# A scan with reciprocals inside its second running products, one mask operation, and its weights split in the early stage

## The chip, the cores and the metric

The kernel runs on one core of a Trainium2 chip. The metric is the device time of one execution, in microseconds. Before the change it is 2709.33 us, the median of 3 runs (2708.7 to 2710.57). TensorE is called PE here, VectorE DVE, ScalarE ACT, GpSimd POOL and SyncE SP; SP issues nearly all DMAs.

## The reference

One layer of a diffusion trunk over 2048 tokens of width 1024, with 256 context tokens ahead: an adaptive norm, an HGRN2 mixer with 8 heads in both directions, and a gated convolution FFN. The change is in the mixer's scan, for a head (cut):

```python
f = lb[d] + (1.0 - lb[d]) * jax.nn.sigmoid(zf)      # k = 1 - f, logf = log f
b = jnp.cumsum(logf, axis=3)                        # over chunks of 64 tokens
qe = q * jnp.exp(b - b_ref)
ke = k * jnp.exp(b_ref - b)
scores = jnp.where(mask, einsum('bhnik,bhnjk->bhnij', qe, ke), 0.0)
o_intra = einsum('bhnij,bhnjv->bhniv', scores, v)
kv = einsum('bhnjk,bhnjv->bhnkv', k * jnp.exp(b_last - b), v)
s = decay[..., None] * s + kv                       # from chunk to chunk
o_inter = einsum('bhnik,bhnkv->bhniv', q * jnp.exp(b), s_start)
```

The latent scans start from the state that the context leaves.

## The kernel before

The program is written out in order, stage by stage, and every engine works through its own instructions in order; a wait at the head of an engine's queue holds up all that is behind it. Work beside the matmuls is put at due times: `tick()` counts one for each three matmuls of a projection (`step`, L937), `at(when, f)` asks for `f` at such a count.

**Early stage** (`early`, L253, to 554.9 us of the trace). Projections of q and v in a scheme with fewer products on quadrants of the token matrix (names such as T2, B12). Matmuls are fp32r in three parts: a number x is split (`split`, L79) into a high half h, a copy on ACT (L80), and the rest l, a subtraction on DVE (L81). From the product `turn_over` on, a generator `ada_rest` (L716) does side work at due times, one step every 7 ticks, 37 steps: it streams rows of the modulation weights through a ring `spare` of four 128 x 1024 slots, multiplies on DVE (L732) and writes rows to DRAM (L746). `spare`, `fraw` (raw factors, loaded at L758 and split later into `rT`, `rB` or `tok`) and `cxt` (the context's modulated tokens, 2 MB, loaded at L1328) are tiles of one tag, "cxt", with a single buffer: each may be filled only when all uses of its forerunner are done. At the last use of T2 the generator is run to its end, and the block B12 is loaded through `fraw` and split into `tok`. The last results of the stage pass a Silu on ACT (L528) and go to DRAM.

**Scan** (`mixer_scan`, L897, 554.9 to 1203 us). Twice (g = 0, 1: the halves of the tokens) over 8 heads; a head has two units of four 128-token tiles, and in g = 0 the context first (`ctx_gates`, L1335). For a unit PE projects both directions' gates (`project`, L951) with weights that `weight` (L1313) brings: in g = 0 it loads the raw 512 KB, splits them (1052 ns on ACT, 1224 on DVE) and stores the 1 MB result in DRAM (`w_d`, L1324); in g = 1 it loads that (L1318). ACT makes F = lb + (1 - lb) sigmoid(z) (L964, L966). Then `factors` (L975), nearly all on DVE, for segments of 32 tokens:

- `S` (L984): running products of F from the front of a segment, one scan for each direction; `d1` holds a 1 at every start of a segment, so that multiply and maximum restart there.
- `ke` (L991, L992): differences of neighbours in S. POOL (L998 to L1004) multiplies segments' totals into the factors `TB` and the decay `sd`, and copies four columns of totals into `TX` (L1017 to L1020).
- `suffix` (L1026): the same scans backwards, into F itself. `rt` (L1028): reciprocals of the segments' totals.
- `rest` (L1030): `qp` = q times F (L1033, L1034), `qi` = qp times TB (the query against the incoming state), `qm` and `km` = qp and ke times TX (scores between segments further apart), half of qp times rt (L1056), `kd` = ke times TB, half of ke times rt (L1059).

`unit_steps` (L1104) then puts on PE, at due times after the unit's projections: `scores` (transposes `tr` of kd and the score matmuls into the PSUM tiles `sc0` and `sc1`; DVE takes them through two masks (L1130) and adds these (L1131) to `at`), `stepped(0)`, `outputs(0)` with `stepped(1)`, and `outputs(1)`. `stepped` multiplies kt and v into one PSUM tile `kv` (L1144), DVE carries the state from it (`states`, then `Sf`, L1147), ACT copies the other direction's half (`sk`, L1150). `outputs` (L1165, L1168) reads states, qi, at and v. The context's `context_state` (L1080) uses the same `kv` buffer. In g = 1 the weights of the output product are scaled on DVE beside this (L1218, eight times, and L1212 once).

Of the kernel before, what the change touches and what calls it, by code (L numbers as in the profile page):

```python
# [11 lines left out]
F32 = mybir.dt.float32  # L12
F32R = mybir.dt.float32r
# [32 lines left out]
def body(ctx, tc, a, out):  # L46
# [206 lines left out]
    def early():  # L253
# [495 lines left out]
        rest = ada_rest()  # L749
# [19 lines left out]
        for i, (g, p, n) in enumerate(todo):  # L769
# [6 lines left out]
            if i == turn_over:  # L776
                for m in range(37):
                    at(clock[0] + 16 + 7 * m, lambda: next(rest, None))
# [118 lines left out]
    def mixer_scan():  # L897
# [11 lines left out]
        mf, mb = [fix.tile([128, 1, 128], F32, name=n) for n in ("mf", "mb")]  # L909
# [7 lines left out]
        for i in range(2):  # L917
            pool.memset(mb[64 * i:64 * i + 64, 0, 64 - 64 * i:128 - 64 * i], 1.0)
        masks = [m.bitcast(U32).to_broadcast([128, UT, 128]) for m in (mb, mf)]
        scs = [ps.tile([128, UT, 128], F32, name=f"sc{d}", tag=f"sc{d}", bufs=1)  # L920
               for d in range(2)]
# [47 lines left out]
        def swish(z, tag):  # L969
            x = gp.tile([128, UT, 128], F32, name=tag, tag=tag, bufs=2)  # L970
# [4 lines left out]
        def factors(h, u, t0, q, v):  # L975
# [19 lines left out]
            TB, TX = [x[2 if u is None else u] for x in (TBs, TXs)]  # L995
# [20 lines left out]
            pool.tensor_copy(decb[:, h, t0:t0 + nt], sd[:, 0])  # L1016
            pool.tensor_copy(TX[:, 0, :, 0], tot[:, 0, :, 1])  # L1017
            pool.tensor_copy(TX[:, 0, :, 3], tot[:, 1, :, 2])
            pool.tensor_copy(TX[:, 1, :, 0], tot[:, 1, :, 1])
            pool.tensor_copy(TX[:, 1, :, 3], tot[:, 0, :, 2])  # L1020
            m = {"sd": sd, "ke": ke, "v": v}

            def suffix():
                for d in range(2):
                    Fr = flat(F[:, d])[:, ::-1]
                    dve.tensor_tensor_scan(Fr, Fr, flat(d1)[:, ::-1], 1.0, OP.mult, OP.max)  # L1026
                m["rt"] = mid("rt", (2, NS))
                dve.reciprocal(m["rt"], S[:, :, :, 32])  # L1028

            def rest():  # L1030
                m["qp"] = qp = mid("qp")
                qv = q.rearrange("p j (c t) -> p (j c) t", t=32)
                dve.tensor_tensor(qp[:, 0], qv, F[:, 0, :, 1:SEG], OP.mult)  # L1033
                dve.tensor_tensor(qp[:, 1], qv, F[:, 1, :, 32:0:-1], OP.mult)  # L1034
# [5 lines left out]
                scaled(qi, qp, TBf[:, 1:3])  # L1040
                qm, km = [mid(n, (UT, 4, 32), bufs=1) for n in ("qm", "km")]
# [1212 lines left out]
```

## Time and profile before

| | |
|---|---|
| median of 3 runs | 2709.33 us |
| the profiled execution's own time | 2706.57 us |
| its span in the trace | 2704.9 us |
| mean granted PE clock | 0.995 |
| matmuls | 15800 |
| early stage / scan / rest, from the trace | 554.9 / 648 / 1502 us |
| a head in g = 0 / a unit in g = 1 | 42.7 / 17.0 to 17.5 us |

A row of the groups by line reads: line, engine, operation, output <- inputs, shapes, count | busy us in all, mean ns of one | idle time of the engine before them and what ended it. A row of the timeline begins with start and duration in us; brackets show how long the engine had stood idle and what released it. A row of the windows has the window's length, then for PE, PEld, DVE, ACT and POOL the busy time and the instructions, then the granted clock, the DMAs' busy share and their GB/s. A row of the waits has the total us, the count and the longest. A row of the DMA issues ends with the KB of one and the median us from issue to landing.

### The profile page before, as it was taken

What the parts mean: (1) busy time and instruction counts of PE and PEld (TensorE: products, weight loads), DVE (VectorE), ACT (ScalarE), POOL (GpSimd) and SP (SyncE); (2) the same over time, 40 slices, a digit from 0 to 9 for tenths busy, and PEclk for the clock granted to TensorE, in tenths of its full rate; (3) what the DMA queues carried; (4) which work ended last, traced back from release to release, by engine and by line L of the source; (5) the groups of instructions that cost most, each with busy time, mean ns of one, the idle gap of its engine ahead of it and who ended that gap; (6) DMA issues with size and microseconds to landing.
All of it is one profiled execution on the core that took longest, in us unless ns stands there. A gap on an engine that the chain in (4) does not pass through costs nothing.

```text
span 2704.9 us, 42255 instructions
## 1 busy us (share of the span) xinstructions
PE 2644.5 (98%) x15800; PEld 2206.3 (82%) x15800; DVE 2106.4 (78%) x3049; ACT 1191.5 (44%) x2051; POOL 651.8 (24%) x936
## 2 busy tenths in 40 slices
PE   6999999999999999999999999999999999999998
PEld 4787788888888888888887888888888888888887
DVE  4856756578887899978887878877877777578896
ACT  4645534433332333335665444443444444333444
POOL 1000222322233322211112443344433440000001
PEclk9999999999999999999999999999999999999999
DMA  8755655364445655548887322227322224988653
GB/s 336 279 199 197 234 200 183 106 248 139 128 159 179 211 184 184 172 151 291 288 319 280 102 86 94 78 79 296 94 94 63 86 86 153 318 272 284 205 180 133
DMA packets 257917, 498.14 MB, mean 184 GB/s; under 512 B 28192, under 2 KB 141232, under 8 KB 249136
## 3 DMA queue, kind: packets, MB, share of 16 engines
q1 hardware_dynamic: 252992, 486.20, 52.9%
q10 hardware_dynamic: 4720, 9.24, 0.9%
q8 instruction: 124, 2.03, 0.3%
q14 instruction: 81, 0.66, 0.1%
HBM read 335.70 MB, written 159.66 MB: 183 GB/s over the span
## 4 chain that ended last, share of the span: by engine, by line
PE 53%; DVE 1%; issue 1%; DMA 0%; ACT 0%; POOL 0%; ACTq 0%; POOLq 0%; DVEq 0%; SPq 0%
PE y L2067 5%; PE y L2066 5%; PE y L2068 5%; PE zc L1465 3%; PE zc L1467 3%; PE zc L1468 3%; PE zd L1468 3%; PE za L1468 3%; PE za L1467 3%; PE zd L1467 3%; PE zd L1465 3%; PE za L1465 3%; PE y L1571 2%; PE y L1569 2%; PE y L1570 2%; PE zb L1467 1%
## 5 line engine op out<-in xcount | busy, mean ns | idle before, releaser
L80 ACT ACTIVATE w<-raw 128x512 fp32r<-128x512 f32 (+1 forms) x286 | 186.1, 656 | 215.1 <-PE zd L1468 75.2
L81 DVE TENSOR_TENSOR w<-raw,w 128x512 fp32r<-128x512 f32 (+1 forms) x286 | 225.8, 793 | 68.6 <-ACT w L80 65.6
L81 DVE TENSOR_TENSOR w<-s,w 128x512 fp32r<-128x512 f32 x195 | 173.9, 897 | 79.8 <-ACT w L80 78.1
L2067 PE MATMUL y<-w,mh 128*128 128x512 f32 x600 | 233.5, 389 | 0.1
L2068 PE MATMUL y<-w,ml 128*128 128x512 f32 x600 | 233.4, 389 | 0.0
L2066 PE MATMUL y<-w,mh 128*128 128x512 f32 x600 | 233.2, 389 | 0.0
L80 ACT ACTIVATE w<-s 128x512 fp32r<-128x512 f32 x195 | 121.8, 630 | 203.9 <-POOL s L220 81.6
L76 POOL TENSOR_TENSOR rs<-rs,mhalf 128x1 f32<-128x1 f32 (+3 forms) x53 | 56.3, 1065 | 446.6 <-DVE rs L75 433.3
L940 PE MATMUL z<-tok,w 128*128 128x512 f32 x352 | 145.8, 414 | 0.0
L1465 PE MATMUL zc<-rT,w 128*128 128x512 f32 x352 | 137.7, 391 | 1.8 <-DMA rT<-rhs1T 1.8
L219 POOL TENSOR_TENSOR s<-raw 128x512 f32<-128x512 f32 x54 | 91.6, 1697 | 195.5 <-DMA raw<-in_w_up_dram 129.5
L941 PE MATMUL z<-tok,w 128*128 128x512 f32 x352 | 138.6, 394 | 0.0
L942 PE MATMUL z<-tok,w 128*128 128x512 f32 x352 | 138.4, 393 | 0.0
L1467 PE MATMUL zc<-rT,w 128*128 128x512 f32 x352 | 137.7, 391 | 0.0
L1468 PE MATMUL zc<-rT,w 128*128 128x512 f32 x352 | 137.5, 391 | 0.0
L2067 PEld LDWEIGHTS y<-w,mh 128*128 128x128 f32 x600 | 112.6, 188 | 23.7 <-DVE w L81 0.6
L2066 PEld LDWEIGHTS y<-w,mh 128*128 128x128 f32 x600 | 112.6, 188 | 23.7 <-ACT w L80 0.3
L984 DVE TENSOR_TENSOR_SCAN S<-F,d 128x528 f32<-128x528 f32 (+1 forms) x80 | 91.5, 1143 | 51.8 <-ACT F L966 51.8
L2068 PEld LDWEIGHTS y<-w,ml 128*128 128x128 f32 x600 | 112.6, 188 | 23.5
L1467 PE MATMUL za<-rB,w 128*128 128x512 f32 x336 | 130.7, 389 | 0.0
L1468 PE MATMUL za<-rB,w 128*128 128x512 f32 x336 | 130.7, 389 | 0.0
L1465 PE MATMUL za<-rB,w 128*128 128x512 f32 x336 | 130.7, 389 | 0.0
(469 smaller groups left out, 7789.0 us busy)
## 6 DMA issues: line engine op xcount, KB each, us to landing
raw<-in_w_up_dram SPq DMA_DIRECT2D x88, 512.0 KB, 3.5
raw<-in_w_in_dram SPq DMA_DIRECT2D x75, 512.0 KB, 5.2
w<-w SPq DMA_DIRECT2D x32, 1024.0 KB, 5.9
lr<-m SPq DMA_DIRECT2D x49, 512.0 KB, 4.8
m<-r SPq DMA_DIRECT2D x66, 256.0 KB, 3.3
spare<-in_w_ada_dram SPq DMA_DIRECT2D x32, 512.0 KB, 5.2
kq<-stash SPq DMA_DIRECT2D x15, 1024.0 KB, 7.4
og<-stash SPq DMA_DIRECT2D x30, 512.0 KB, 4.9
```

Source lines behind the costliest of these rows:

```text
L80: i = act.activation(h, src, AF.Copy)
L81: j = dve.tensor_tensor(l, src, h.bitcast(F32), OP.subtract)
L219: eng.tensor_tensor(s1, a21, a22, OP.add)
L940: pe.matmul(z, w[:, 0, k], h, start=k == 0, stop=False, skip_group_check=True)
L941: pe.matmul(z, w[:, 0, k], l, start=False, stop=False, skip_group_check=True)
L942: pe.matmul(z, w[:, 1, k], h, start=False, stop=k == KT - 1, skip_group_check=True)
L1465: pe.matmul(o, w[:, 0, k], r[:, :, 0, k], start=start and k == 0, stop=False, skip_group_check=True)
L1467: pe.matmul(o, w[:, 0, k], r[:, :, 1, k], start=False, stop=False, skip_group_check=True)
L1468: i = pe.matmul(o, w[:, 1, k], r[:, :, 0, k], start=False, stop=k == 3, skip_group_check=True)
L2066: pe.matmul(z, lh, rh, start=start, stop=False, skip_group_check=True)
L2067: pe.matmul(z, lh, rl, start=False, stop=False, skip_group_check=True)
L2068: pe.matmul(z, ll, rh, start=False, stop=stop, skip_group_check=True)
```

## The change

Four parts. (1) The second scan no longer starts every segment at 1: a tile `d2` holds at each start the reciprocal of a neighbour's total for half of the segments, and the result goes to S instead of F, so the later product of half of qp with rt falls away. POOL copies these reciprocals from `rt` into `d2`, so `rt` is now made before the second scan. (2) The scaled query copies `qm` go; the scores between distant segments read `qp` of the other direction, and `km` takes products of totals (POOL multiplies two of the four columns of TX, which were copies). (3) The two masks and two PSUM tiles become one of each, and one masked copy of 128 x 1024. (4) The weights of the scan's gates are split in the early stage by a second generator `weights_rest` behind `ada_rest`, through the same `spare` ring, and stored to `w_d`; the scan loads them in both halves. The generator is advanced 54 times, every 5.25 ticks. Beside these, `kd` of the context becomes a step of its own with earlier due times, and `q` has one buffer instead of two.

```diff
-        rest = ada_rest()
+        def weights_rest():
+            todo = [(h, ty) for h in range(NH) for ty in (2, 1)]
+            ring = spare[0]
+            def load(n):
+                if n < len(todo):
+                    h, ty = todo[n]
+                    sp.dma_start(ring[:, n % 2], a["w_in"][h, ty])
+            load(0)
+            yield
+            hl = ring[:, 2:4]
+            for n, (h, ty) in enumerate(todo):
+                load(n + 1)
+                w = hl.bitcast(F32R)
+                split(w[:, 0], w[:, 1], ring[:, n % 2])
+                sp.dma_start(w_d[h][ty - 1], hl.rearrange("p i n -> p (i n)"))
+                yield
+        def all_rest():
+            yield from ada_rest()
+            yield from weights_rest()
+        rest = all_rest()
 ...
             if i == turn_over:
-                for m in range(37):
-                    at(clock[0] + 16 + 7 * m, lambda: next(rest, None))
+                for m in range(54):
+                    at(clock[0] + 16 + 5 * m + m // 4, lambda: next(rest, None))
 ...
-        mf, mb = [fix.tile([128, 1, 128], F32, name=n) for n in ("mf", "mb")]
+        mbf = fix.tile([128, 2, 1, 128], F32, name="mbf")
+        mb, mf = [mbf[:, i] for i in range(2)]
 ...
-        scs = [ps.tile([128, UT, 128], F32, name=f"sc{d}", tag=f"sc{d}", bufs=1)
-               for d in range(2)]
+        masks = mbf.bitcast(U32).to_broadcast([128, 2, UT, 128])
+        sc2 = ps.tile([128, 2, UT, 128], F32, name="sc", tag="sc", bufs=1)
+        scs = [sc2[:, d] for d in range(2)]
 ...
-        ABs = [fix.tile([128, UT, 128], F32, name=f"AB{d}") for d in range(2)]
+        AB = fix.tile([128, 2, UT, 128], F32, name="AB")
 ...
-        TXs = [fix.tile([128, 2, n, 4], F32, name=f"TX{i}") for i, n in enumerate((UT, UT, 2))]
-        for m in (*Fs, *TBs, *TXs):
+        TXs = [fix.tile([128, UT, 4], F32, name=f"TX{i}") for i in range(2)]
+        for m in (*Fs, *TBs):
 ...
-        for m in ABs:
-            pool.memset(m, 0.0)
+        d2 = fix.tile([128, 2, NS, SEG], F32, name="d2")
+        pool.memset(d2, 0.0)
+        pool.memset(d2[:, :, :, 0:1], 1.0)
+        pool.memset(AB, 0.0)
 ...
         def swish(z, tag):
-            x = gp.tile([128, UT, 128], F32, name=tag, tag=tag, bufs=2)
+            x = gp.tile([128, UT, 128], F32, name=tag, tag=tag, bufs=1)
 ...
-            TB, TX = [x[2 if u is None else u] for x in (TBs, TXs)]
+            TB = TBs[2 if u is None else u]
 ...
-                scaled(kd, ke, TBf[:, 0:4:3])
-                return kd, sd
+                return kd, sd, lambda: scaled(kd, ke, TBf[:, 0:4:3])
+            TX = TXs[u]
 ...
-            pool.tensor_copy(TX[:, 0, :, 0], tot[:, 0, :, 1])
-            pool.tensor_copy(TX[:, 0, :, 3], tot[:, 1, :, 2])
-            pool.tensor_copy(TX[:, 1, :, 0], tot[:, 1, :, 1])
-            pool.tensor_copy(TX[:, 1, :, 3], tot[:, 0, :, 2])
+            rt = mid("rt", (2, NS))
+            dve.reciprocal(rt, S[:, :, :, 32])
+            pool.tensor_copy(d2[:, 0, 2:NS:2, 0], rt[:, 0, 1:NS - 1:2])
+            pool.tensor_copy(d2[:, 1, 1:NS:2, 0], rt[:, 1, 0:NS:2])
+            pool.tensor_copy(TX[:, :, 1], tot[:, 1, :, 2])
+            pool.tensor_copy(TX[:, :, 2], tot[:, 0, :, 1])
+            pool.tensor_tensor(TX[:, :, 0], tot[:, 1, :, 1], tot[:, 1, :, 2], OP.mult)
+            pool.tensor_tensor(TX[:, :, 3], tot[:, 0, :, 1], tot[:, 0, :, 2], OP.mult)
 ...
-                    dve.tensor_tensor_scan(Fr, Fr, flat(d1)[:, ::-1], 1.0, OP.mult, OP.max)
-                m["rt"] = mid("rt", (2, NS))
-                dve.reciprocal(m["rt"], S[:, :, :, 32])
+                    dve.tensor_tensor_scan(flat(S[:, d])[:, ::-1], Fr, flat(d2[:, d])[:, ::-1],
+                                           1.0 if d else rt[:, 0, NS - 1:NS], OP.mult, OP.max)
 ...
-                dve.tensor_tensor(qp[:, 0], qv, F[:, 0, :, 1:SEG], OP.mult)
-                dve.tensor_tensor(qp[:, 1], qv, F[:, 1, :, 32:0:-1], OP.mult)
+                dve.tensor_tensor(qp[:, 0], qv, S[:, 0, :, 1:SEG], OP.mult)
+                dve.tensor_tensor(qp[:, 1], qv, S[:, 1, :, 32:0:-1], OP.mult)
 ...
-                scaled(qi, qp, TBf[:, 1:3])
-                qm, km = [mid(n, (UT, 4, 32), bufs=1) for n in ("qm", "km")]
-                m.update(qm=qm, km=km)
-                scaled(qm[:, :, 0:2], seg(qp[:, 0])[:, :, 0:2], TX[:, 0, :, 0:2])
-                scaled(qm[:, :, 2:4], seg(qp[:, 1])[:, :, 2:4], TX[:, 0, :, 2:4])
-                scaled(km[:, :, 0:2], seg(ke[:, 1])[:, :, 0:2], TX[:, 1, :, 0:2])
-                scaled(km[:, :, 2:4], seg(ke[:, 0])[:, :, 2:4], TX[:, 1, :, 2:4])
-                def halves(x, first):
-                    c = x[:, 0, first]
+                c = TBf[:, 1, 0]
+                dve.tensor_tensor(qi.rearrange("p d (s g) t -> p d s (g t)", g=2),
+                                  qp.rearrange("p d (s g) t -> p d s (g t)", g=2),
+                                  bass.AP(tensor=c.tensor, offset=c.offset,
+                                          ap=[list(c.ap[0]), [NS + 1, 2], [2, NS // 2], [0, 64]]),
+                                  OP.mult)
+                m["km"] = km = mid("km", (UT, 4, 32), bufs=1)
+                scaled(km[:, :, 0:2], seg(ke[:, 1])[:, :, 0:2], TX[:, :, 0:2])
+                scaled(km[:, :, 2:4], seg(ke[:, 0])[:, :, 2:4], TX[:, :, 2:4])
+                def halves(x):
+                    c = x[:, 0, 0]
 ...
-                                   ap=[list(c.ap[0]), [(NS + 1 - 2 * first) * step, 2],
+                                   ap=[list(c.ap[0]), [(NS + 1) * step, 2],
 ...
-                dve.tensor_tensor(halves(qp, 1), halves(qp, 1), halves(m["rt"], 1), OP.mult)
 ...
-                made_last.append(dve.tensor_tensor(halves(ke, 0), halves(ke, 0), halves(m["rt"], 0),
+                made_last.append(dve.tensor_tensor(halves(ke), halves(ke), halves(rt),
 ...
-                ke, qp, qm, km = [m[n] for n in ("ke", "qp", "qm", "km")]
+                ke, qp, km = [m[n] for n in ("ke", "qp", "km")]
 ...
-                        score(0, s, km[:, s, j], j, qm[:, s, qc], qc)
+                        score(0, s, km[:, s, j], j,
+                              qp[:, 1 - j // 2, 4 * s + qc.start:4 * s + qc.stop], qc)
 ...
-                for d in range(2):
-                    dve.copy_predicated(ABs[d], masks[d], scs[d])
-                made_last.append(dve.tensor_tensor(at_, *ABs, OP.add).ins)
+                dve.copy_predicated(AB, masks, sc2)
+                made_last.append(dve.tensor_tensor(at_, AB[:, 0], AB[:, 1], OP.add).ins)
 ...
-                if g and ty < 3:
+                if ty < 3:
 ...
-                    if ty < 3:
-                        sp.dma_start(w_d[h][ty - 1], flat)
 ...
-                context = factors(h, None, None, None, None)
-                for dt, f in zip((8, 17), context_state(h, *context, cv)):
+                kd, sd, keys = factors(h, None, None, None, None)
+                for dt, f in zip((5, 9, 12), (keys, *context_state(h, kd, sd, cv))):
 ...
-                q = gp.tile([128, UT, 128], F32, name="q", tag="q", bufs=2)
+                q = gp.tile([128, UT, 128], F32, name="q", tag="q", bufs=1)
 ...
             def out_gate(hh, u):
-                keep_gate(hh, t0[u], swish(project(weight(g, hh, 4), u), "q"))
+                keep_gate(hh, t0[u], swish(project(weight(g, hh, 4), u), ("q", "kdc")[hh % 2 ^ u]))
 ...
-            unit(0, (6, 11, 19, 21, 26, 30))
+            unit(0, (6, 11, 19, 21, 24, 27) if last else (6, 11, 19, 21, 26, 30))
 ...
-            unit(1, (6, 11, 19, 21, 24, 26) if last else (6, 11, 19, 21, 26, 30))
+            unit(1, (5, 9, 17, 19, 21, 23) if last else (6, 11, 19, 21, 26, 30))
```

How the instructions move. Lines of the changed kernel stand some 30 higher in the scan. The first place is ACT where the early stage ends and the scan begins. Before, from the splits of `fraw` into `tok` to the first sigmoid of the scan:

```order
L80 ACTIVATE tok<-fraw 128x512 [waits DMAHW6_49]
L80 ACTIVATE tok<-fraw 128x512 x3
L80 ACTIVATE w<-raw 128x512 [waits DVE_49,PE_49] x2
L528 ACTIVATE out<-out 128x512 [waits DMAHW0_49,DVE_49]
L80 ACTIVATE w<-raw 128x1024 [waits DMAHW1_49]
L528 ACTIVATE out<-out 128x512 [waits DMAHW2_49,DVE_49]
L80 ACTIVATE w<-raw 128x1024 [waits DMAHW5_49,PE_49]
L528 ACTIVATE out<-out 128x512 [waits DMAHW3_49,DVE_49,Activation_49]
L528 ACTIVATE out<-out 128x512 [waits DMAHW4_49,DVE_49,Activation_49]
L528 ACTIVATE out<-out 128x512 [waits DMAHW7_49,DVE_49,Activation_49]
L528 ACTIVATE out<-out 128x512 [waits DMAHW0_49,DVE_49,Activation_49]
L964 ACT_TABLE_LOAD [waits PE_49]
```

And now (`spare<-spare` is the high half of a split weight):

```order
L80 ACTIVATE spare<-spare 128x1024 [waits DMAHW5_49,DMAHW2_49,Activation_49]
L528 ACTIVATE out<-out 128x512 [waits DMAHW3_49,DVE_49]
L528 ACTIVATE out<-out 128x512 [waits DMAHW7_49,DVE_49,Activation_49]
L80 ACTIVATE spare<-spare 128x1024 [waits DMAHW6_49,DMAHW3_49,Activation_49]
L80 ACTIVATE spare<-spare 128x1024 [waits DMAHW7_49,DMAHW4_49,DVE_49]
L80 ACTIVATE spare<-spare 128x1024 [waits DMAHW5_49,DMAHW0_49,DVE_49]
L80 ACTIVATE spare<-spare 128x1024 [waits DMAHW6_49,DMAHW0_49,DVE_49]
L80 ACTIVATE tok<-fraw 128x512 [waits DMAHW5_49]
L80 ACTIVATE tok<-fraw 128x512 x3
L991 ACT_TABLE_LOAD [waits PE_49]
```

The splits of `tok` moved from ahead of the last six Silus to behind them, and behind the last four of the sixteen weights; each of these waits for two DMAs, the load of its raw half and the store of the weight before. The second place is SP's queue there. Before, `fraw`, `cxt` and the context's values `v` stood like this, with stores of results and weights between:

```order
L758 DMA fraw<-part_124 128x4x512 [waits DMAHW6_49,DMAHW4_49,DVE_49]
L529 DMA q_173<-out 128x512 [waits DMAHW7_49,Activation_49]
L529 DMA q_168<-out 128x512 [waits DMAHW0_49,Activation_49]
L1321 DMA raw<-in_w_in_dram 128x1024 [waits DMAHW1_49,Pool_49]
L529 DMA q_176<-out 128x512 [waits DMAHW2_49,Activation_49]
L529 DMA q_180<-out 128x512 [waits DMAHW3_49,Activation_49]
L529 DMA q_188<-out 128x512 [waits Activation_49]
L1321 DMA raw<-in_w_in_dram 128x1024 [waits DMAHW5_49,DVE_49]
L1328 DMA cxt<-cxt 128x4096 [waits DMAHW6_49,DVE_49]
```

And now (L766 is the store of a split weight, L757 the load of a raw one):

```order
L1108 DMA v<-v_127 128x512 [waits DMAHW3_49]
L1349 DMA w<-w_199 128x2048 [waits DMAHW4_49]
L766 DMA w_208<-spare 128x2048 [waits DMAHW5_49,DVE_49]
L757 DMA spare<-in_w_in_dram 128x1024 [waits DMAHW6_49]
L1349 DMA w<-w_198 128x2048 [waits DMAHW7_49]
L766 DMA w_211<-spare 128x2048 [waits DMAHW0_49,DVE_49]
L1108 DMA v<-v_128 128x512 [waits DMAHW1_49]
L1108 DMA v<-cv_159 128x256 [waits DMAHW2_49]
L1240 DMA g_9299<-m_row_60 128x1024 [waits DMAHW3_49]
L766 DMA w_210<-spare 128x2048 [waits DMAHW4_49,DVE_49]
L782 DMA fraw<-part_124 128x4x512 [waits DMAHW5_49,DMAHW6_49,DMAHW4_49,DMAHW0_49]
L1357 DMA cxt<-cxt 128x4096 [waits DMAHW5_49,DVE_49]
```

`fraw` and `cxt` moved behind the stores of the last weights and behind loads for the scan. The third place is DVE in a unit of the second half of the scan with an output weight to scale, from the second direction's `ke` to the states of the unit before. Scans are listed as SCALAR_TENSOR_TENSOR, and d is `d1` or `d2`. Before:

```order
L992 TENSOR_TENSOR ke<-S 128x16x32 [waits DVE_49]
L1026 SCALAR_TENSOR_TENSOR F_4704<-F_4704,d_4701 128x528
L1028 RECIPROCAL rt<-S 128x32
L1034 TENSOR_TENSOR qp<-q,F_4704 128x512 [waits DVE_49]
L1010 TENSOR_TENSOR qm<-qp,TX_4712 128x4x64 [waits PE_49,Pool_49]
L1130 COPY_PREDICATED AB_4707<-mb,sc_4697 128x512 [waits PE_49]
L1130 COPY_PREDICATED AB_4708<-mf,sc_4698 128x512 [waits PE_49]
L1010 TENSOR_TENSOR qi<-qp,TB_4709 128x1024 [waits DMAHW0_49,DMAHW7_49,DVE_49,Pool_49]
L1131 TENSOR_TENSOR at<-AB_4707,AB_4708 128x512 [waits DVE_49]
L1218 SCALAR_TENSOR_TENSOR spare<-spare,vec,g_9356 128x1024
L1147 SCALAR_TENSOR_TENSOR states<-Sf,sd,kv 128x128 [waits PE_49]
```

And now:

```order
L1019 TENSOR_TENSOR ke<-S 128x16x32 [waits DVE_49]
L1045 RECIPROCAL rt<-S 128x32
L1057 SCALAR_TENSOR_TENSOR S<-F_4766,rt,d_4781 128x528 [waits Pool_49]
L1057 SCALAR_TENSOR_TENSOR S<-F_4766,d_4781 128x528 [waits Pool_49]
L1161 COPY_PREDICATED AB<-mbf,sc 128x1024 [waits PE_49]
L1063 TENSOR_TENSOR qp<-q,S 128x512 [waits DMAHW1_49,DVE_49]
L1162 TENSOR_TENSOR at<-AB 128x512 [waits DVE_49]
L1249 SCALAR_TENSOR_TENSOR spare<-spare,vec,g_9299 128x1024 [waits DMAHW0_49]
L1178 SCALAR_TENSOR_TENSOR states<-Sf,sd,kv 128x128 [waits PE_49]
L1064 TENSOR_TENSOR qp<-q,S 128x512
L1178 SCALAR_TENSOR_TENSOR states<-states,sd,kv 128x128 [waits DVE_49]
```

Both second scans now stand together behind `rt` and wait for POOL; the masked copy, `at` and the states of the unit before stand behind them, where only one scan stood, and `qi` moved behind the states.

More of the change, by code (lines that the diff above doesn't have):

```diff
@@ L918, in mixer_scan @@
             pool.memset(mb[64 * i:64 * i + 64, 0, 64 - 64 * i:128 - 64 * i], 1.0)
-        masks = [m.bitcast(U32).to_broadcast([128, UT, 128]) for m in (mb, mf)]
-        scs = [ps.tile([128, UT, 128], F32, name=f"sc{d}", tag=f"sc{d}", bufs=1)
-               for d in range(2)]
+        masks = mbf.bitcast(U32).to_broadcast([128, 2, UT, 128])
+        sc2 = ps.tile([128, 2, UT, 128], F32, name="sc", tag="sc", bufs=1)
+        scs = [sc2[:, d] for d in range(2)]
         for sc in scs:
```

## The prediction

> **What bounds the kernel now.** I read the page's busy times first, then the windows by stage, then PE's waits in the scan, then the timeline at the place where the early stage hands over to the scan.
>
> ```profile
> PE 2644.5 (98%) x15800; PEld 2206.3 (82%) x15800; DVE 2106.4 (78%) x3049; ACT 1191.5 (44%) x2051; POOL 651.8 (24%) x936
> 250.00:555.00 305.00, 302.55 (x1376) 247.34 (x1375) 194.53 (x260) 130.19 (x230) 81.81 (x65) 0.99 0.55 185
> 555.00:890.00 335.00, 323.50 (x3265) 283.01 (x3264) 279.99 (x441) 116.12 (x213) 103.79 (x248) 1.00 0.51 166
> 890.00:1203.00 313.00, 306.95 (x3226) 264.47 (x3225) 280.56 (x447) 105.69 (x209) 84.54 (x207) 0.99 0.53 170
> PE kv L1144 <- DVE Sf L1092: 5.6, 7, 0.8
> PE o L1165 <- DVE states L1147: 5.0, 8, 1.1
> PE o L1165 <- ACT oi L1264: 3.1, 2, 1.9
> PE kv L1144 <- ACT sk L1150: 2.7, 9, 0.4
> ```
>
> PE is busy 98% of the span. The change leaves its matmuls alone in number and size, so the time can fall only by PE's waits and rise only by new ones. The second to fourth rows are the windows (length, busy PE, PEld, DVE, ACT, POOL): early stage, first and second half of the scan. In the scan DVE is busy 84% and 90%, yet PE stands still little: the last four rows are all its larger waits there (us in total, times, longest), 16.4 us. Removing vector work therefore cannot win more than some 20 us, 0.7%, matmul start-up included.
>
> ```profile
> 554.70 0.39 PE L520 MATMUL zc<-rT,w 128*128 128x512 f32 x1
> 554.93 0.28 PE L940 MATMUL z<-cxt,w 128*128 128x256 f32 x1
> 511.91 0.58 SPq L758 DMA_DIRECT2D fraw<-part  x1
> 533.97 2.18 ACT L80 ACTIVATE tok<-fraw 128x512 fp32r<-128x512 f32 x4
> 534.70 1.89 DVE L81 TENSOR_TENSOR tok<-fraw,tok 128x512 fp32r<-128x512 f32 x3
> 538.42 0.32 SPq L1328 DMA_DIRECT2D cxt<-cxt  x1
> 555.90 0.63 ACT L528 ACTIVATE out<-out 128x512 f32<-128x512 f32 x1 [2.09 <-DVE out L559]
> ```
>
> These are the hand-over: the scan's first matmul reads `cxt` and starts 0.23 us behind the last of the early stage. It has no wait, because `fraw` was loaded at 511.9, split into `tok` from 534.0, and `cxt` was requested at 538.4, 16.5 us ahead. `spare`, `fraw` and `cxt` share one buffer (tag "cxt", one copy), so each waits for the last user of the one before.
>
> **The split weights in the early stage.** Sixteen splits now use `spare`: raw halves in slots 0 and 1, the result always in slots 2 and 3. Split n may not overwrite these before store n-1 has landed. A cycle is thus ACT's part, DVE's part, and a 1 MB store:
>
> ```profile
> L80 ACT ACTIVATE w<-raw 128x1024 fp32r<-128x1024 f32 x16 | 16.8, 1052 | 0.0
> L81 DVE TENSOR_TENSOR w<-raw,w 128x1024 fp32r<-128x1024 f32 x16 | 19.6, 1224 | 9.6 <-ACT w L80 8.9 <-DMA v<-v 0.6
> w<-w SPq DMA_DIRECT2D x16, 1024.0 KB, 4.8
> fraw<-part SPq DMA_DIRECT2D x8, 1024.0 KB, 6.7
> tok<-tokB SPq DMA_DIRECT2D x4, 2048.0 KB, 8.8
> lat<-lat SPq DMA_DIRECT2D x16, 512.0 KB, 4.0
> ```
>
> 1.05 + 1.22 + 4.8 = 7.1 us. The generator is advanced every 5.25 ticks; a tick is three matmuls of 0.227 us, so every 3.6 us: the ring cannot keep that pace. What is left over stands where ACT's new order puts it: the last four splits come behind the stage's last Silu (before at 555.90), and behind them, in this order, `fraw`, the `tok` splits, `cxt`, and PE's first scan matmul, with nothing else for PE to do. From 555.9: four cycles, 28.3 us; `fraw`, 6.7; the `tok` splits, 0.6 on ACT and then four of 0.62 on DVE, 3.1; `cxt`, 2 MB like `tok<-tokB`, 8.8. That is 46.9 us, to 602.8: PE starts 47.9 us late. Each of some fourteen hand-offs costs more: 0.18 us lay between ACT's first `tok` split (533.97, a quarter of 2.18) and DVE's at 534.70; I take 0.15, so 2.1. And PE will have stood still:
>
> ```profile
> 1145.80 0.49 PE L1165 MATMUL o<-states,qi 128*128 128x128 f32 x2 [1.92 <-ACT oi L1264]
> 1147.87 0.63 PE L942 MATMUL z<-tok,w 128*128 128x512 f32 x1
> 1144.70:1148.20 3.50, 2.40 (x11) 2.21 (x12) 3.15 (x5) 2.93 (x10) 1.02 (x1) 0.76 0.00 0
> 1148.20:1152.00 3.80, 3.80 (x95) 3.03 (x98) 3.14 (x6) 1.61 (x5) 3.50 (x10) 0.77 0.37 104
> ```
>
> After a wait of only 1.92 us a matmul takes 0.63 us and not 0.39, and the granted clock is 0.76 and 0.77 in the two windows behind (3.5 x 0.24 + 3.8 x 0.23 = 1.7 us lost). I charge the long wait one such stretch. Sum for the ring: **+52 us**. Bounds: +44 if a store lands in 4.0, as half the size does in the last row, and hand-offs and clock cost 1.4 together; +68 if each cycle is 8.4 us (stores at 5.9, the median of all 32 `w<-w`, and 0.2 for hand-offs) and the ring, started near 470, already holds up ACT ahead of its last Silus, which delays the tail too.
>
> The Trainium skill, "DMA: Bandwidth & Descriptors", section "Anatomy of one DMA", fits a transfer at 2.0 us plus bytes over 436 GB/s, which is 4.4 us for 1 MB and 6.8 for 2 MB, for another way of issuing; by it the ring would cost about 6 us less, as an estimate. The rows of this trace are longer and I keep them.
>
> **The scan, what goes.** Per unit of two per head, 32 in all:
>
> ```profile
> L1010 DVE TENSOR_TENSOR qm<-qp,TX 128x256 f32<-128x256 f32 x64 | 26.3, 420 | 1.0
> L1130 DVE COPY_PREDICATED AB<-mf,sc 128x512 f32<-128x512 uint32 x32 | 23.1, 723 | 0.0
> L1056 DVE TENSOR_TENSOR qp<-qp,rt 128x512 f32<-128x512 f32 x32 | 21.9, 684 | 0.0
> L1026 DVE TENSOR_TENSOR_SCAN F<-F,d 128x528 f32<-128x528 f32 x64 | 80.1, 1252 | 0.0
> ```
>
> DVE loses two `qm` (0.84 us) and the product by `rt` (0.68). Two masks of 0.72 become one of 128x1024, not in the trace: between 0.72 and 1.44, I take 1.25, since L81's 128x1024 takes 1.22 against 0.68 for L1056's 128x512. The second scans stay, now with fp32 `d2` in place of bf16 `d1`: not in the trace either. At 1.25 us for 528 elements against 0.68 for a product of 512 they are paced by the recurrence and not by reading, so I take no change; twice as long is the far bound, and would cost another 1.25 in each. The sixteen weight splits (16.8 us of ACT, 19.6 of DVE) leave the first half. All this lies beside PE's 98%; only where it stands ahead of a `states` does it count.
>
> **The scan, what comes.** The second scans need `d2`, which POOL copies from `rt` at the end of its chain, so DVE waits for POOL where it never did, and behind that wait in DVE's order stand the previous unit's mask, `at` and `states`, for which PE waits. A unit of the second half, with the output weights' scaling:
>
> ```profile
> 1006.87 1.26 DVE L984 TENSOR_TENSOR_SCAN S<-F,d 128x528 f32<-128x528 f32 x1 [1.00 <-ACT F L966]
> 1008.17 0.69 DVE L992 TENSOR_TENSOR ke<-S 128x512 f32<-128x512 f32 x1
> 1009.95 0.32 DVE L1028 RECIPROCAL rt<-S 128x32 f32<-128x32 f32 x1
> 1014.04 1.28 DVE L1218 SCALAR_TENSOR_TENSOR spare<-spare,vec,g 128x1024 f32<-128x1024 f32 x1
> 1015.83 0.34 DVE L1147 SCALAR_TENSOR_TENSOR states<-states,sd,kv 128x128 f32<-128x128 f32 x1
> 1015.96 0.39 PE L1168 MATMUL o<-v,at 128*128 128x128 f32 x2
> 1016.64 1.16 PE L1144 MATMUL kv<-v,kt 128*128 128x128 f32 x8 [0.30 <-ACT sk L1150]
> 1008.19 0.72 POOL L998 COPY TB<-S 128x8 f32<-128x8 f32 x1 [5.03 <-DVE S L984]
> 1011.37 0.21 POOL L1004 TENSOR_TENSOR TB<-TB,S 128x8 f32<-128x8 f32 x1
> 1011.54 0.21 POOL L1001 TENSOR_TENSOR sd<-TB,S 128x8 f32<-128x8 f32 x1
> 1011.81 0.19 POOL L1016 COPY decb<-sd 128x4 f32<-128x4 f32 x1
> ```
>
> POOL's chain took 3.8 us here (1008.19 to 1012.00). Its first took 0.72 us beside `ke`; late ones follow each other every 0.17 us (1011.37 to 1011.54). In the new order DVE has only `ke` and `rt` left before the wait, so it is free at 1009.1, and POOL runs alone: ten operations of 0.17 from there, `d2` ready at 1010.8. Then two scans, 1013.3; mask, 1014.5; `qp` half, 1015.1; `at`, 1015.7; the scaling, 1016.9; `states`, the other `qp` half, `states`, 1018.1; `sk` on ACT 0.4, and PE's `kv` at 1018.55 against 1016.64, **1.9 us later**. It comes back in every unit, since the first scan waits for PE's projection of that unit. In a unit without the scaling DVE is 1.2 earlier before and now: `kv` at 1017.35, where PE would have been ready at 1016.18 (1015.96 and two short matmuls), so 1.2 us remain. Nine units with, six without: 17.1 + 7.2 = **+24 us**. Ends: 0 if `d2` is there when DVE is free (1.7 us less in each, 1016.85), and +40 if POOL needs its 3.8 as before (1.1 more in fifteen units).
>
> A page of the Trainium skill bears on which of the two it is: "SBUF — State Buffer", section "Who interferes with whom", says that a two-input VectorE instruction shuts out a GpSimd instruction that reads SBUF for its whole length. The rows agree (0.72 us beside `ke`, 0.21 late in the chain), and by it POOL is fast just when DVE waits for it: +24; without it the 3.8 would hold: +40.
>
> In the first half the wait of 5.6 us (7 times 0.8, the context's `kv` buffer) goes, since the context's steps now come nine matmuls, 2.0 us, before the unit's. The POOL wait brings something like it at the first unit's second step: the 1.9 of above less the 1.2 of a weight split (L81) that stood in that chain, 0.7 in each of eight heads, 5.6. I take 0, from -11 (5.6 + 5.0, all of this half's waits gone) to +15 (the full 1.9 in eight heads). The ready weights come as 1 MB loads in place of 0.5 MB loads and 1 MB stores, requested a head ahead: nothing.
>
> **Sum.** Profiled execution 2706.57 (span 2704.9): + 52 + 24 + 0 = 2782.6. The median of the runs is 2.8 above it, so **2785 us**.
>
> **Rivals.** (1) POOL's wait is hidden, and the first half gains its 10 us: 2709 + 52 - 10 = 2751. For it: DVE loses 1.7 us a unit. Against: the new order puts nothing between `rt` and the second scans. (2) The ring runs at 8.4 us, +68, or POOL at 3.8: 2801. For it: 5.9 is the median of all such transfers. (3) **Faster**: the single result buffer does not hold up the splits, so the ring ends ahead of the Silus, and the waits of the scan go: 2709 - 20 = 2689. It decides at a cycle of about 3.9 us (from 470 to the 530 at which `fraw` must be asked for, over sixteen); the fastest such store alone takes 4.8, and four splits stand behind the last Silu, so hardly. (4) The ring's tail is short and the scan repays it: 2709.
>
> **How the numbers follow.** My forecast 0.47, (1) 0.24, (2) 0.22, (3) 0.04, (4) 0.03. The range takes in (1) with the ring at its lower bound, 2743, and (2) with some of both of its causes, 2815. About 0.2% is what a measurement of this kernel can tell from no change: faster 0.04, same 0.03, slower 0.93.
>
> **What would show it.** Right: PE idle for 45 to 60 us just behind the last early product, released by `cxt`; four splits of `spare` about 7 us apart behind the last Silu; then DVE idle 1.5 to 2 us before the second scan, released by POOL, and `kv` waits of 1 to 2 us in the second half. Wrong: `cxt` requested before the early stage ends; stores that land in 3 us; splits in pairs; second scans of 2.5 us; or `d2` ready as early as `rt`.

## The result, and the profile after

The changed kernel takes 2806.78 us, the median of 4 runs (2804.56 to 2812.57), against 2709.01: the ratio is 1.0364, with a 95% interval of 1.0346 to 1.0381. The profiled execution took 2804.56 us, its span is 2802.6. That is 98 us more; the prediction had 76, and its range (2743 to 2815) holds the time. A unit's time is taken on PE, from its first transposes to those of the next unit.

The page's first row and the windows of the changed kernel by stage (length; busy PE, PEld, DVE, ACT, POOL; granted clock, DMA share, GB/s): early stage, the gap behind it, first and second half of the scan. The last row is the second half in the kernel before.

```profile
PE 2669.8 (95%) x15800; PEld 2219.7 (79%) x15800; DVE 2086.5 (74%) x2921; ACT 1191.1 (42%) x2051; POOL 610.4 (22%) x998
250.00:560.00 310.00, 303.86 (x1384) 247.42 (x1382) 217.97 (x267) 137.25 (x237) 85.89 (x67) 1.00 0.68 230
560.00:612.10 52.10, 0.00 (x0) 0.01 (x1) 9.82 (x12) 7.16 (x10) 2.06 (x6) 0.53 0.78 294
612.10:946.20 334.10, 325.42 (x3152) 283.19 (x3153) 241.22 (x359) 100.12 (x195) 75.43 (x266) 0.99 0.40 123
946.20:1303.50 357.30, 330.46 (x3337) 279.39 (x3335) 265.56 (x384) 106.20 (x211) 64.56 (x244) 0.96 0.49 154
885.80:1202.80 317.00, 310.95 (x3336) 267.89 (x3335) 283.24 (x450) 107.51 (x212) 85.75 (x208) 0.99 0.54 174
```

PE does the same 15800 matmuls, and DVE lost 20 us of work. There are two losses: a hole of 52 us in which PE does nothing, and a second half of 357.3 us where the same stretch took 317.0 before (885.8 to 1202.8). The first half nearly kept its pace: a head takes 43.06 us from one context product to the next, against 42.73.

The hole is the ring. First ACT (a split weight is `spare<-spare`), then SP, then the wait that ends it, from the timeline of the changed kernel:

```profile
558.54 1.06 ACT L80 ACTIVATE spare<-spare 128x1024 fp32r<-128x1024 f32 x1 [2.78 <-DMA w<-spare]
...
561.54 0.63 ACT L528 ACTIVATE out<-out 128x512 f32<-128x512 f32 x1 [1.42 <-DVE out L559]
565.95 1.06 ACT L80 ACTIVATE spare<-spare 128x1024 fp32r<-128x1024 f32 x1 [3.78 <-DMA w<-spare]
573.73 1.06 ACT L80 ACTIVATE spare<-spare 128x1024 fp32r<-128x1024 f32 x1 [6.73 <-DMA w<-spare]
581.79 1.06 ACT L80 ACTIVATE spare<-spare 128x1024 fp32r<-128x1024 f32 x1 [7.00 <-DMA w<-spare]
589.11 1.06 ACT L80 ACTIVATE spare<-spare 128x1024 fp32r<-128x1024 f32 x1 [6.26 <-DMA w<-spare]
600.85 2.19 ACT L80 ACTIVATE tok<-fraw 128x512 fp32r<-128x512 f32 x4 [10.68 <-DMA fraw<-part]
```

```profile
591.45 0.32 SPq L766 DMA_DIRECT2D w<-spare  x1
595.39 0.57 SPq L782 DMA_DIRECT2D fraw<-part  x1
604.03 0.33 SPq L1357 DMA_DIRECT2D cxt<-cxt  x1
```

```profile
612.13 0.55 PE L967 MATMUL z<-cxt,w 128*128 128x256 f32 x1 [52.32 <-DMA cxt<-cxt]
```

Each split waits for the store of the one before, 7.7 us apart; the last store is requested at 591.45, `fraw` at 595.39 behind it, `cxt` at 604.03 behind the splits of `tok`, and PE starts at 612.13 instead of 554.93.

The second half shows the wait for POOL, and what stands behind it. DVE in a unit without an output weight to scale, then POOL and PE there:

```profile
966.93 1.26 DVE L1011 TENSOR_TENSOR_SCAN S<-F,d 128x528 f32<-128x528 f32 x1 [3.40 <-ACT F L993]
...
968.84 0.35 DVE L1045 RECIPROCAL rt<-S 128x32 f32<-128x32 f32 x1
970.67 1.32 DVE L1057 TENSOR_TENSOR_SCAN S<-F,rt,d 128x528 f32<-128x528 f32 x1 [1.48 <-POOL d L1046]
971.90 1.23 DVE L1057 TENSOR_TENSOR_SCAN S<-F,d 128x528 f32<-128x528 f32 x1
973.05 1.29 DVE L1161 COPY_PREDICATED AB<-mbf,sc 128x1024 f32<-128x1024 uint32 x1
...
976.02 0.35 DVE L1178 SCALAR_TENSOR_TENSOR states<-Sf,sd,kv 128x128 f32<-128x128 f32 x1
976.28 1.23 DVE L1071 TENSOR_TENSOR qi<-qp,TB 128x1024 f32<-128x1024 f32 x1
977.42 0.35 DVE L1178 SCALAR_TENSOR_TENSOR states<-states,sd,kv 128x128 f32<-128x128 f32 x1
```

```profile
970.03 0.22 POOL L1028 TENSOR_TENSOR sd<-TB,S 128x8 f32<-128x8 f32 x1
...
970.44 0.20 POOL L1046 COPY d<-rt 128x7 f32<-128x7 f32 x1
```

```profile
976.42 0.49 PE L1196 MATMUL o<-states,qi 128*128 128x128 f32 x2 [0.37 <-DVE states L1178]
978.24 1.16 PE L1175 MATMUL kv<-v,kt 128*128 128x128 f32 x8 [1.10 <-ACT sk L1181]
```

DVE idles 1.48 us for `d2`; PE then waits twice in the unit. Such a unit takes 19.0 us where it took 16.85. `qi`, 1.2 us, stands between the two states. In such a unit of the kernel before it stood ahead of both, and PE had no wait above 0.1 us:

```profile
904.31 1.26 DVE L984 TENSOR_TENSOR_SCAN S<-F,d 128x528 f32<-128x528 f32 x1 [1.70 <-ACT F L966]
...
909.76 1.20 DVE L1010 TENSOR_TENSOR qi<-qp,TB 128x1024 f32<-128x1024 f32 x1
910.88 0.68 DVE L1131 TENSOR_TENSOR at<-AB,AB 128x512 f32<-128x512 f32 x1
911.48 0.34 DVE L1147 SCALAR_TENSOR_TENSOR states<-Sf,sd,kv 128x128 f32<-128x128 f32 x1
```

### The profile page after: what moved, and what is told of

Same layout as the page of the kernel before. It is cut to its first block, busy times and chain, and to the rows that moved or that the text cites. A ratio compares the mean times of both kernels' runs of the same rounds, so it can differ in the third digit from the quotient of the medians.

```text
span 2802.6 us, 42181 instructions
## 1 busy us (share of the span) xinstructions
PE 2669.8 (95%) x15800; PEld 2219.7 (79%) x15800; DVE 2086.5 (74%) x2921; ACT 1191.1 (42%) x2051; POOL 610.4 (22%) x998
## 4 chain that ended last, share of the span: by engine, by line
PE 53%; DVE 3%; issue 1%; DMA 1%; ACT 1%; POOL 0%; POOLq 0%; DVEq 0%; ACTq 0%; SPq 0%
PE y L2096 5%; PE y L2095 5%; PE y L2097 5%; PE zc L1494 3%; PE zc L1496 3%; PE zc L1497 3%; PE zd L1497 3%; PE za L1497 3%; PE zd L1496 3%; PE za L1496 3%; PE zd L1494 3%; PE za L1494 3%; PE y L1598 2%; PE y L1600 2%; PE y L1599 2%; PE zb L1497 1%
## 5 line engine op out<-in xcount | busy, mean ns | idle before, releaser
L80 ACT ACTIVATE w<-raw 128x512 fp32r<-128x512 f32 (+1 forms) x270 | 169.2, 632 | 207.8 <-PE zd L1497 75.3
L81 DVE TENSOR_TENSOR w<-raw,w 128x512 fp32r<-128x512 f32 (+1 forms) x270 | 211.7, 788 | 50.8 <-ACT w L80 48.4
L967 PE MATMUL z<-tok,w 128*128 128x512 f32 x352 | 149.6, 425 | 0.0
L969 PE MATMUL z<-tok,w 128*128 128x512 f32 x352 | 141.5, 402 | 0.0
L968 PE MATMUL z<-tok,w 128*128 128x512 f32 x352 | 140.8, 400 | 0.0
```

The source lines that it names most:

```text
L80: i = act.activation(h, src, AF.Copy)
L81: j = dve.tensor_tensor(l, src, h.bitcast(F32), OP.subtract)
L967: pe.matmul(z, w[:, 0, k], h, start=k == 0, stop=False, skip_group_check=True)
L968: pe.matmul(z, w[:, 0, k], l, start=False, stop=False, skip_group_check=True)
L969: pe.matmul(z, w[:, 1, k], h, start=False, stop=k == KT - 1, skip_group_check=True)
```

## The experiments

Ratios are to the kernel before, run beside them; the times are medians.

**One part at a time.** e1 is the change without the split weights of the early stage, e2 the kernel before with them alone.

```diff
 e1 (from the changed kernel):
-        rest = all_rest()
+        rest = ada_rest()        # and its 37 steps, every 7 ticks
 ...
-                if ty < 3:
+                if g and ty < 3:
 ...
+                    if ty < 3:
+                        sp.dma_start(w_d[h][ty - 1], flat)
 e2 (from the kernel before): the same lines the other way round, and weights_rest
```

> The change without its fourth part: the weights of the gates are split in the scan as before, one running-product, one-mask scan as after. Theory A (the ring of the early stage costs its own 57 us and has nothing to do with the scan): scan starts at 555 as before, the time is 2807 - 57 = 2750, units of the second half stay at 19.0 to 20.7 us. Rival B (the late start or the missing weight splits also slow the scan, by transfers or by the clock): units go back towards 17.0 to 17.5 and the time to 2720 or less.

> The kernel before with the fourth part alone. Theory A: PE's first matmul of the scan waits some 52 us for cxt and starts near 612; the first half of the scan may win up to 10 us from the missing splits: 2757 to 2766. Rival B (the ring costs mainly in company with the new scan): below 2740.

e1: 2747.37 us, ratio 1.0143 (1.0128 to 1.0158). e2: 2767.55, ratio 1.0217 (1.0200 to 1.0234). 38.6 and 58.8 us add up to 97.4 of the whole's 98: the parts do not need each other. e2's row of PE's first product, and e1's second half:

```profile
612.14 0.55 PE L964 MATMUL z<-cxt,w 128*128 128x256 f32 x1 [51.85 <-DMA cxt<-cxt]
```

```profile
887.20:1245.80 358.60, 330.15 (x3337) 279.33 (x3336) 265.86 (x383) 106.16 (x211) 65.05 (x244) 0.96 0.48 154
```

PE starts the scan at 612.14, within 0.01 us of the changed kernel, behind a wait of 51.85 us where that had 52.32; and e1 has the same slow half, 358.6 us against 357.3. Theory A holds for both, a little above its range in e2: there a head of the first half takes 43.26 us, more than the 42.73 of before, so that the splits that left the scan won nothing at all. In such a head `outputs` waits 1.07 us for a state, where it waited 0.55 before.

**Doses of the ring.** e8 is e2 with only ten weights in the early stage; e10 is e2 with two results in flight.

```diff
 e8:
-            todo = [(h, ty) for h in range(NH) for ty in (2, 1)]
+            todo = [(h, ty) for h in range(5) for ty in (2, 1)]
 ...
-                if ty < 3:
+                if ty < 3 and (g or h < 5):
 e10:
-                    sp.dma_start(ring[:, n % 2], a["w_in"][h, ty])
+                    sp.dma_start(ring[:, n % 2 * 2 + 1], a["w_in"][h, ty])
 ...
-                split(w[:, 0], w[:, 1], ring[:, n % 2])
+                split(w[:, p], w[:, p + 1], ring[:, p + 1])      # p = n % 2 * 2
```

> As e2 (2767.5), but only the first ten of the sixteen weights (heads 0 to 4) are split in the early stage, the others in the scan as before. Theory A (a chain of split, store, split of 7.7 us each that ends too late): six cycles, 46 us less, PE waits some 6 to 12 us for cxt: 2718 to 2728. Rival (what PE waits for is the load of fraw and cxt as such, or anything that does not grow with the number): 2750 or more.

> As e2 (2767.5), with two results in flight: each raw half is split in place in its own pair of ring slots (high half beside it), so split n waits for store n-2 and its own load. Theory A: two weights in load 5 + 2.3 + store 4.9, some 6 us a weight instead of 7.7, and two splits instead of four behind the last Silu: 20 to 30 us less, 2738 to 2748. Rival (transfers are the limit, not the wait for the one result): within 8 us of e2.

e8: 2722.74 us, ratio 1.0051 (1.0037 to 1.0065); PE waits 10.03 us for `cxt`. Six weights less took 44.8 us, 7.5 us each: the loss grows by one cycle a weight, once the stage's slack is used up. e8 also shows what the ready weights do to a head of the first half: 43.23 us with them, 42.73 in the later heads, whose weights are split in the scan. e10: 2751.61, ratio 1.0160 (1.0144 to 1.0175). 16 us less than e2, under theory A's 20 to 30 and over the rival's 8: with two results in flight nearly every wait of a split is one for its own load, which takes longer here than in my estimate:

```profile
spare<-in_w_in_dram SPq DMA_DIRECT2D x16, 512.0 KB, 5.7
```

So the single result is a part of the cycle, the load the next thing behind it. At the end e10 did not have two in flight: the last load was requested at 569.43, when the store requested at 564.53 had landed, and the last split came 13.9 us behind the one before it. Pairs of splits had been 13 us apart before, so two in flight would have brought that split some 7 us earlier, an estimate, and the time into theory A's range.

**The wait for POOL.** e3 lets POOL copy `d2` first; e5 does so and gives POOL a copy of the totals.

```diff
 e3 (from e1):
+                dve.reciprocal(rt, S[:, :, :, 32])
+                pool.tensor_copy(d2[:, 0, 2:NS:2, 0], rt[:, 0, 1:NS - 1:2])
+                behind = [pool.tensor_copy(d2[:, 1, 1:NS:2, 0], rt[:, 1, 0:NS:2]).ins]
 ...
+            with tc.issue_after(behind[0]):      # the same around POOL's chain
 e5 (from e3):
+                tt = mid("tt", (2, NS))
+                dve.tensor_copy(tt, S[:, :, :, 32])
 ...
-            tot = S[:, :, :, 32].rearrange("p d (s g) -> p d s g", g=4)
+            tot = (S[:, :, :, 32] if u is None else tt).rearrange("p d (s g) -> p d s g", g=4)
```

> As e1, but POOL copies the reciprocals into d2 first and makes its factors behind. Theory C (DVE's wait for POOL, 1.5 us a unit, is what PE pays for): that wait falls to 0.4 us, units of the second half fall by about 1.1 us in 22, 24 us, and the half-clock stretches (some 13 us) mostly go: about 2715 where e1 has 2750. Rival D (the cost is the order: both second scans ahead of the states, qi between the states): the wait falls, but units stay above 18.5 and the time above 2738.

> As e3, and DVE copies the segments' totals out of S (one more operation, some 0.3 us), from which POOL makes its factors. Theory E (e3 got slower because the second scan writes over S and so waits until POOL has read all totals, not only for d2): DVE's wait for POOL falls under 0.6 us, units of the second half from 19.0-20.7 to some 18.0, and the half-clock stretches mostly go: 2710 to 2718. Rival D (the order of the scans, the states and qi): units stay above 18.5, above 2735.

e3 was a miss, and the most useful one: 2771.4 us, ratio 1.0229 (1.0214 to 1.0244), 24 us slower than e1. The wait did not fall, it grew, and its releaser changed. e3's timeline, DVE and POOL:

```profile
927.16 1.32 DVE L1039 TENSOR_TENSOR_SCAN S<-F,rt,d 128x528 f32<-128x528 f32 x1 [2.10 <-POOL sd L1013]
```

```profile
925.25 0.20 POOL L1002 COPY d<-rt 128x8 f32<-128x8 f32 x1
...
926.91 0.21 POOL L1013 TENSOR_TENSOR sd<-TB,S 128x8 f32<-128x8 f32 x1
```

`d2` was ready at 925.45, and DVE still waited until `sd`, POOL's last reader of S, had ended: the second scan writes over S. In the changed kernel `sd` ends at 970.25, 0.4 us ahead of `d2`, so its trace names only `d2`. e5 takes both away:

```profile
908.68 0.12 DVE L1002 COPY tt<-S 128x32 f32<-128x32 f32 x1
909.06 1.33 DVE L1041 TENSOR_TENSOR_SCAN S<-F,rt,d 128x528 f32<-128x528 f32 x1 [0.26 <-POOL d L1003]
```

```profile
886.90:1214.80 327.90, 314.52 (x3337) 267.72 (x3337) 267.19 (x401) 105.32 (x211) 84.45 (x244) 1.00 0.52 168
```

2716.9 us, ratio 1.0028 (1.0017 to 1.0039): theory E, inside its range. The half falls from 358.6 to 327.9 us, units to 17.9, and the clock is back at 1.00.

**What is left in a unit.** e4 takes the reciprocals out of the second scan again (the other parts stay); e6 and e7 put `qi` behind both states, in e5 and in e4; e9 makes `qi` first, as before the change; e11 and e12 move a unit's second step.

```diff
 e4 (from e1):
-                    dve.tensor_tensor_scan(flat(S[:, d])[:, ::-1], Fr, flat(d2[:, d])[:, ::-1],
-                                           1.0 if d else rt[:, 0, NS - 1:NS], OP.mult, OP.max)
+                    dve.tensor_tensor_scan(Fr, Fr, flat(d1)[:, ::-1], 1.0, OP.mult, OP.max)
 ...
+                dve.tensor_tensor(halves(qp, 1), halves(qp, 1), halves(rt, 1), OP.mult)
 e6 (from e5) and e7 (from e4), in stepped:
+                if p == 0:
+                    with tc.issue_after(last):      # the second state
+                        m["make_qi"]()
 e9 (from e4): this product behind km, and
+                scaled(qi, qp, TBf[:, 1:3])
 e11 (from e9), for both units:
-            unit(0, (6, 11, 19, 21, 24, 27) if last else (6, 11, 19, 21, 26, 30))
+            unit(0, (6, 11, 19, 21, 24, 27) if last else (6, 11, 19, 21, 25, 30))
 e12 (from e9), for both units: in place of that 25
+                                                   25 if g and not 2 <= h < 6 else 26
```

> As e1 without the reciprocals in the second scan: the scan of before into F from d1, half of qp times rt as a product again (ahead of qi), still no qm and one mask. Theory C: no wait for POOL, DVE 1 us shorter a unit than before, units of the second half 16.9 to 17.2: 2700 to 2709. Rival D: the one-mask operation and the order of qi cost as well, units of 17.5 or more: 2715 to 2725.

> As e5, with qi made behind both states of the first step. Theory F (in units without an output weight to scale qi stands between the two states and costs PE its 1.15 us): these fourteen units fall by 1.0 to 1.1 more, some 14 us below e5: about 2700. Rival (PE is held elsewhere, qi is hidden): within 4 us of e5.

> As e4 (2705 there, units 17.8), with qi behind both states. Theory F: units of the second half 17.0 to 17.2, some 12 us less: 2692 to 2697. Rival (hidden): 2703 to 2707.

> As e4, but qi is made as in the kernel before (from qp ahead of its product with rt), and that product comes behind km. Theory G (what counts is only what stands between the arrival of the second direction's F and the second state: in e4 the product with rt, 0.6 us, and a longer mask; here 0.6 less): units of the second half 16.9 to 17.3 against 17.8 in e4, the first half keeps its 41.3 a head: 2690 to 2697, faster than both kernels. Rival (units are held by something else, such as DVE's total work): 17.7 or more, 2703 to 2707.

> As e9 (2701; plain units 17.6), with the second step of a unit put at 25 ticks instead of 26: on DVE its first state then stands ahead of the next unit's second scan and not behind it. Theory G (only what stands ahead of a state counts): the 0.5 us wait of PE in plain units goes, these units come to 16.9 to 17.1, 4 to 6 us in all: 2695 to 2698. Rival (the kv product, now 0.7 us earlier on PE, waits as long for the states of the first step): 2700 to 2704.

> As e9, with the second step at 25 ticks only in those units of the second half that scale no output weight (in e11 these came to 17.1 and the others rose to 18.2). Theory G: plain units 17.1, units with the scaling 17.6, the first half at 41.3 a head as in e9: 3 to 4 us under e9, 2696 to 2699. Rival (run-to-run differences of start and end cover it): 2699 to 2703.

e4: 2705.29 us, ratio 0.9985 (0.9976 to 0.9995): the time of theory C, but not by its way. Heads of the first half fall to 41.3 us, which is where the time is won, and units of the second half stay at 17.8 (16.85 before), so in these rival D was right. e6 and e7: 2751.08, ratio 1.0158 (1.0143 to 1.0173), and 2722.76, ratio 1.0056 (1.0044 to 1.0069), 34 and 17 us slower than e5 and e4. Theory F fell, and so did the rivals that held `qi` to be hidden. e7's waits of PE:

```profile
PE o L1174 <- DVE qi L1051: 29.0, 22, 2.0
```

Behind the states `qi` comes too late for `outputs`, which needs it at once. e9: 2701.03, ratio 0.9974 (0.9963 to 0.9984), the lowest time of all and 0.3% under the kernel before. It wins in the first half, 41.3 us a head against 42.7, and misses the 2690 to 2697 of theory G, since units are 17.6. On DVE the next unit's second scan stood ahead of the second step's state there, and PE waited 0.52 us:

```profile
911.93 0.49 PE L1162 MATMUL o<-states,qi 128*128 128x128 f32 x2 [0.52 <-DVE states L1144]
```

e11 turns that order: units without scaling fall to 17.1 as expected, those with it rise from 17.6 to 18.3. There PE comes to `outputs` earlier, but the first state stands behind the scaling as before, and `outputs` gets a wait that e9 has not:

```profile
1012.81 0.49 PE L1162 MATMUL o<-states,qi 128*128 128x128 f32 x2 [0.56 <-DVE states L1144]
```

The `kv` behind it waits 0.30 us in both runs, so it is not `kv`, as the rival had it. e11 takes 2709.25, ratio 1.0005 (0.9996 to 1.0014). e12 was to mix the two: 2703.46, ratio 0.9977 (0.9968 to 0.9986), no gain over e9 that these runs can tell. It did not change what it was meant to, though: by the trace the earlier step reached two plain units (17.1), while two ahead of them stayed at 17.7, and one with the scaling had it (18.3). So e12 does not decide between theory G and its rival. All three of theory G's times were missed; that a unit follows what stands ahead of its states was seen in e9 and e11.

## Why the prediction was right, and where it was short

The time is 22 us above the 2785 that I forecast: 8 of it lies in the ring and its clock, 16 in the second half, 1 in the first, and the stages behind the scan took 3 less. My lower bound for the ring, +44, comes to +46 by the terms given for it.

**The ring: +52 predicted, the hole itself measured 57.2 and with the clock some 60.** The mechanism was right step by step. The cycle was 7.7 us (7.1 and hand-offs); four splits stood behind the last Silu. Three terms differ. The last Silu came at 561.54 instead of 555.90. Half of this is PE's waits for ACT once the splits had begun there (451.64), which I had kept for the upper bound. PE's waits from 440 to 612 us, apart from the one for `cxt`; the kernel before has none from 440 us on:

```profile
PE za L517 <- ACT u L546: 1.5, 2, 1.0
PE za L517 <- ACT out L528: 1.2, 1, 1.2
```

The other half need not come from the ring: in the runs without it the scan starts between 553.7 and 557.9, against 554.9 in the kernel before. The thirteenth split, the first of the four, then still waited 3.8 us for the store before it. `fraw` and `cxt` were faster than my rows, 5.5 and 8.1 us against 6.7 and 8.8. The clock behind the hole cost more than one stretch:

```profile
612.10:617.60 5.50, 5.47 (x26) 5.50 (x27) 0.00 (x0) 0.00 (x0) 0.00 (x0) 0.52 0.00 0
```

5.5 us at 0.52, 2.6 us lost against 1.7. The fit in the Trainium skill, "DMA: Bandwidth & Descriptors", section "Anatomy of one DMA", for another way of issuing, gives 4.4 us for 1 MB and 6.8 for 2 MB; the stores landed in 4.9 (median) and `cxt` in 8.1, so keeping the rows was right.

**The second half: +24 predicted, +40.3 measured (357.3 against 317.0).** The wait for POOL came as worked out (1.7 us predicted, 1.48 measured), and so did the chain behind it. e5, with 0.26 us of that wait left, gets 1.1 us back in every unit and the full clock with it; 1.1 and 0.5 us remain there in units without and with the scaling. By size, what I lacked most is the clock, 11 us, which is worked out below. The step of the working that failed is "In a unit without the scaling DVE is 1.2 earlier before and now", which priced such units at 1.2 us. They lost 2.2. In their order `qi` stands between the two states, 1.2 us in the place where the others have the scaling; I had read the order of a unit with scaling alone. That `qi` is the reason is read from the order; no run shows it, and e6 and e7, which take `qi` out of this place, made units longer. Units with the scaling lost 1.6, near the 1.9 predicted, but not by `kv` alone: there `outputs` waits 0.97 us for the first state and `kv` 0.57. With the clock set aside the fourteen regular units lost 25.7 us, near the 24 predicted; that is partly luck, since one kind cost 1.0 more each and the other 0.3 less. The term for the clock: a unit of 20.6 us beside one of 19.0, the windows of the changed kernel.

```profile
984.30:1003.30 19.00, 17.53 (x186) 14.86 (x185) 14.07 (x20) 5.35 (x10) 3.65 (x14) 1.00 0.42 130
1003.30:1023.90 20.60, 19.13 (x186) 16.16 (x185) 14.07 (x20) 5.34 (x10) 3.79 (x14) 0.92 0.44 120
```

The two do the same work; in the second the clock is 0.92, 1.6 us. Seven units are such, some 11 us, and none in e5. I had charged one such stretch, at the hole.

**The wait for POOL, its cause.** I named `d2` alone, and e3 was built on that. It shows that S written in place is a second reason: with `d2` early, DVE waited for `sd` instead, and longer.

**The first half: 0 predicted, +0.3 us a head measured.** The 5.6 us for the context's `kv` went, as forecast, and waits of like size came. The term that I put at "nothing" is the ready weights: e1's heads take 42.4 us and e2's 43.26 against 42.73, so the new scan won 0.3 us a head and the ready weights cost 0.5.

**POOL alone or beside DVE.** POOL's operations took 0.2 us from the end of `ke` to `d2`, as the section "Who interferes with whom" of "SBUF — State Buffer" in the Trainium skill leads one to expect where DVE idles, and the 3.8 us chain of rival (2) did not come. In e5, where DVE's scan runs beside POOL's chain from 909.06 on, the second of these two copies takes 1.17 us, though the first, begun beside the scan too, still takes 0.20:

```profile
909.09 0.20 POOL L1012 COPY TB<-tt 128x8 f32<-128x8 f32 x1
909.22 1.17 POOL L1016 COPY TB<-tt 128x8 f32<-128x8 f32 x1
```

**Rivals.** (1) needed POOL's wait to be hidden, and DVE's wait of 1.48 us speaks against it; (3) needed a ring that its single result does not hold up, (4) a short tail, and the hole and e8 speak against both. The 2801 of (2) is nearer to the 2807 measured than my 2785. But its chain of 3.8 us did not come, and the ring cost some 60 and not 68; the second half did lose the 40 that (2) had for it, from other causes.

## What to carry to other kernels

A ring with a single result buffer takes a full store per step, and a load that shares its buffer waits for the last one: count the cycle against the time that the ring is given, and put what the next stage needs ahead of it. Before work is taken off a busy engine, ask whether what is left waits for a slower one: here DVE lost work and gained a wait ahead of all that PE waits for. A tile written in place is a wait for all its readers, and the trace names only the last one.

## What the hardware showed beside this

- In the second half the granted clock fell to one half for 3.4 us at a time, by the trace's clock records, mostly 20.5 us apart, in units where PE's longest wait was 1.1 us and its two waits made 1.5; in e5, with one wait of 0.7 us at most in a regular unit, it did not. The length of the wait alone does not decide it: in e7 each regular unit of the second half has one wait of 1.5 us, and there it did not fall either. The Trainium skill, "TensorE: Matmul & The Clock Gate", section "HAM oscillation — how this bites in real kernels", tells of such an alternation for gaps above some 3.4 us; here it came with gaps a third as long, and what decides stays open.
- The second scan with an fp32 `d2` takes 1.24 and 1.32 us, as with the bf16 `d1` (1.25). The masked copy of 128x1024 takes 1.30, against twice 0.72: the one mask saves 0.14 us.
